# Gate columns of six feed-forward groups as seven quarter products instead of eight

## The chip, the cores and the metric

One core of one Trainium2 chip runs the whole layer as one program. The metric is device time in microseconds, the median of three runs.

## The reference, cut to what matters

One decoder layer on 512 tokens of width 1024 in float32: a modulated norm, two attention mixers that share an input projection, an output projection, and then a gated feed-forward part. The change touches the last part alone:

```
h = rms_norm(x, g_ffn_norm) * (1 + sc_f) + sh_f            # 512 x 1024
g_ff, u_ff = split(h @ w_gate_up, 2)                       # w_gate_up: 1024 x 5632
x = x + gt_f * ((silu(g_ff) * u_ff) @ w_down)              # 2816 hidden columns
```

`gt_f` is one of six vectors made from the condition `c`: `silu(c) @ w_mod + b_mod`, split in six.

## The kernel before, in words

Every float32 product is made of three matmuls in the `fp32r` type: each operand x is split into a high part (a cast, on ScalarE, ACT below) and a low part (x minus the high part, on VectorE, DVE below), and `mm3` (line 166) adds high times high, high times low and low times high in PSUM. `main3` (line 550) is `mm3` followed by `step()`, which lets the recording layer put in work of other engines.

**The order.** The program is written once, by Python generators ("tasks") and a small cost table (`Clocks`) that estimates when each engine comes to each instruction. `step()` puts in a piece of a task when the estimate says that its inputs are ready. What comes out is one fixed order for each engine; on the chip every engine runs its own order from front to back and waits on semaphores. So an instruction that waits holds up all that stands behind it on its engine, whether that needs the same thing or not.

**The feed-forward part.** The 2816 hidden columns are 11 groups of 256, `gi` = 0 to 10. A group has gate columns and up columns, each as two blocks of 128 features (f = 0, 1 gate, f = 2, 3 up) by 512 tokens, features on the partitions. The weights of a group come in four chunks of 256 rows (`gate_up_src`, line 1162; gate and up side by side): `wload` (line 176) loads a chunk into a tile `st` (three of them), ACT casts it to `wh`, DVE subtracts to `wl` (`split` inside `drive`, line 584; three `wh` and three `wl` tiles). A chunk is loaded as soon as the tile that it takes comes free, some two chunks ahead of TensorE. TensorE (PE) runs 24 matmuls of 512 tokens for each chunk: 4 blocks, 2 slices of 128 rows, 3 matmuls. Group 0 (`first_up`) is cut along the tokens, 256 at a time. Its weights were split early, into `O` tiles. Even groups collect in four PSUM banks `psacc`, odd ones in `pss`, two `pstr` and `pspv`.

**After a group** (`up_done`, line 1314) ACT takes silu of the gate blocks and DVE multiplies the up blocks in. `combine` (line 1268) then makes what the down projection needs, which was already done with seven products for eight (sums and differences of 256-token halves): four blocks for the first half of the products, kept in `g`, `K` or `O` tiles, and three for the second half, which are written to HBM as `second{gi}` by a DMA on the POOL queue and fetched later.

**The vector gt_f** is made beside groups 1 and 2 (`gtf_task`, line 1379; `mod_rows`, line 1009; `column_sums`, line 934), in two halves of 512 columns. Each half loads eight row blocks of `w_mod` in four DMAs into the same three `st` tiles that the weights use, and DVE adds them up in eight instructions (`cg<-st,cs,cg`). The sum is split into high and low parts, `gu` tiles, and two matmuls with a vector of ones add over the partitions (`pstr<-gu,oner`). These two matmuls have a fixed place in PE's order, between matmuls of the fourth chunk of group 1 (first half) and of the third chunk of group 2 (second half of the vector). If the `gu` tiles are late there, PE waits.

The functions that the change touches:

Of the kernel before, what the change touches and what calls it, by code (L numbers as in the profile page):

```python
# [115 lines left out]
def layer(ctx, tc, x, vecs, w_mod, w_in, gvecs, w_br_dsa, w_br_moba, w_out, w_gate_up, w_down, cosh, sinh, cosi, sini, out):  # L117
# [430 lines left out]
    emptied_next = [False]  # L548

# [34 lines left out]
    def drive(chunks, ws, ahead=2):  # L584
# [17 lines left out]
        def prep(c):  # L602

            early = c < len(chunks) and chunks[c][3]

            def load_next():
                if c + 1 < len(chunks) and chunks[c + 1][3]:
                    yield room("st"), lambda: block_room()
# [87 lines left out]
    sqj = cp.tile([P, HD], F32, name="sqj")  # L696
# [570 lines left out]

    def combine(gi, a0, a1):
# [10 lines left out]
        ve.tensor_tensor(out=s4, in0=a1[:, first], in1=a0[:, other], op=ALU.subtract)  # L1279
        if gi < 4:  # L1280
            yield a0, s13, room("g", 4)
            tiles = [t("g", [P, 2, 256], F32R) for _ in range(4)]
            ha, la, hb, lb = tiles
        else:
            tag = "K" if gi < 8 else "O"
            yield a0, s13, room(tag)
            tiles = [t(tag, [P, 4, 2, 256], F32R)]
# [8 lines left out]
        pair_tiles[gi] = tiles  # L1296
        pairs[gi] = {"A11": (ha[:, 0], la[:, 0]), "S2": (ha[:, 1], la[:, 1]), "S1": (hb[:, 0], lb[:, 0]),
                     "S3": (hb[:, 1], lb[:, 1])}
        ready.add(f"pair{gi}")
# [12 lines left out]
        ready.add(f"stored{gi}")  # L1312

    def up_done(gi):
        half = {}
# [49 lines left out]

    units = first_up()
    chunks.append((None, units[:4], ("h2_0", "h2_1"), None))
    chunks.append((None, units[4:], ("h2_2", "h2_3"), None))
    for gi in range(1, NF // 2):
        chunks += group([gate_up_src(gi, k2) for k2 in range(4)], 512, other_four if gi % 2 else four(),  # L1370
                        feat_mm(lambda k: (h2[k // 4][:, k % 4, :], h2[2 + k // 4][:, k % 4, :])), [0, 2, 1, 3],
                        up_done(gi))
# [51 lines left out]
    def earliest(*tags):  # L1424
        return lambda: min([min(free[tag]) for tag in tags if free[tag]], default=None)

# [15 lines left out]
    def split_first_half(loaded):  # L1442
# [3 lines left out]
        t2 = t(min((tag for tag in ("sc", "s") if free[tag]), key=lambda tag: min(free[tag])), [P, 512])  # L1446
# [40 lines left out]
    def second_task():  # L1487

        for q in range(NPAIR):
            yield (f"stored{NPAIR - 1}", "down",  # L1490
                   lambda: min([min(free[tag]) for tag in ("K", "O") if free[tag]], default=None))
            tag = min((tag for tag in ("K", "O") if free[tag]), key=lambda tag: min(free[tag]))
            x = t(tag, [P, 6, 256], F32R)
            pool_dma(x, second_acts[q])
            pairs[q] = {n: (x[:, a], x[:, 3 + a]) for a, n in enumerate(("A12", "A22", "S4"))}
# [162 lines left out]

    for second, load_of, split_of in ((False, load_first_half, split_first_half), (True, load_second_half, split_second_half)):
# [3 lines left out]
    with tc.manual_schedule(engines=engines):  # L1663
# [27 lines left out]
        spawn(gtf_task())  # L1691
        spawn(second_task(), slack=8.0, rank=0, on=(DVE,))
# [49 lines left out]
```

## Time and profile before

| | |
|---|---|
| median of 3 runs | 772.85 us (772.16 to 773.34) |
| the profiled execution | 771.89 us, of which the span from the first to the last instruction is 770.1 us |
| PE busy | 762.7 us, 99% of the span |
| weight loads (PEld) | 633.7 us, beside PE |
| DVE busy | 543.9 us, 71% |
| ACT busy | 394.4 us, 51% |
| granted TensorE clock | 1.00 throughout, the 2.4 GHz level |
| DMA | 126.59 MB, 164 GB/s over the span |

The profiled execution is one run with the hardware profiler; its span is the time between the first and the last instruction, and its own device time is 1.8 us more. A "busy" time adds up instructions that overlap only once. Matmuls are pipelined, so a single matmul's duration in a row is longer than the time that it adds; the time that one adds is read from the stretch of many in a row.

### The profile page before, as it was taken

What the parts mean: (1) busy time and instruction counts of PE and PEld (TensorE: products, weight loads), DVE (VectorE), ACT (ScalarE), POOL (GpSimd) and SP (SyncE); (2) the same over time, 40 slices, a digit from 0 to 9 for tenths busy, and PEclk for the clock granted to TensorE, in tenths of its full rate; (3) what the DMA queues carried; (4) which work ended last, traced back from release to release, by engine and by line L of the source; (5) the groups of instructions that cost most, each with busy time, mean ns of one, the idle gap of its engine ahead of it and who ended that gap; (6) DMA issues with size and microseconds to landing.
All of it is one profiled execution on the core that took longest, in us unless ns stands there. A gap on an engine that the chain in (4) does not pass through costs nothing.

```text
span 770.1 us, 10321 instructions
## 1 busy us (share of the span) xinstructions
PE 762.7 (99%) x3668; PEld 633.7 (82%) x3668; DVE 543.9 (71%) x1035; ACT 394.4 (51%) x835; POOL 48.3 (6%) x65
## 2 busy tenths in 40 slices
PE   8999999999999999999999999999999999999998
PEld 7787888888788887888888988888888888888886
DVE  6974889989799796337857277645444445897797
ACT  6763786779777756643435333333323323554341
POOL 2000012011111000000000000000000000012100
PEclk9999999999999999999999999999999999999999
DMA  9976352542035455433440257533444443479992
GB/s 319 333 227 228 84 170 78 165 134 58 29 83 193 149 163 194 151 109 123 139 149 1 83 185 251 178 124 101 132 150 124 150 150 138 160 256 381 331 319 83
DMA packets 84559, 126.59 MB, mean 164 GB/s; under 512 B 8976, under 2 KB 49240, under 8 KB 84508
## 3 DMA queue, kind: packets, MB, share of 16 engines
q1 hardware_dynamic: 80460, 105.75, 43.2%
q0 software_dynamic: 4048, 20.19, 7.5%
q8 instruction: 29, 0.48, 0.3%
q14 instruction: 22, 0.18, 0.1%
HBM read 112.28 MB, written 13.64 MB: 164 GB/s over the span
## 4 chain that ended last, share of the span: by engine, by line
PE 95%; SPq 2%; DVE 1%; DMA 1%; issue 0%; ACT 0%; ACTq 0%
PE psacc L110 62%; PE pstr L110 15%; PE pspv L110 9%; PE pss L110 9%; SPq L183 1%; DMA K<-in_w_mod_dram 1%; SPq L212 1%; DVE V L110 1%; DVE s L110 1%; SPq L221 0%; ACT gu L110 0%; ACT H L110 0%; SPq L205 0%; ACT acol L110 0%; ACT mcol L110 0%
## 5 line engine op out<-in xcount | busy, mean ns | idle before, releaser
L110 PE MATMUL psacc<-H,wh 128*128 128x512 f32 x576 | 182.8, 398 | 0.0
L110 DVE TENSOR_TENSOR wl<-st,wh 128x1024 fp32r<-128x1024 f32 (+1 forms) x110 | 128.5, 1168 | 61.1 <-ACT wh L110 60.9
L110 ACT CAST wh<-st 128x1024 fp32r<-128x1024 f32 (+1 forms) x110 | 110.4, 1005 | 76.3 <-PE psacc L110 32.6
L110 PE MATMUL psacc<-wh,H 128*128 128x512 f32 x384 | 126.5, 400 | 0.9 <-ACT H L110 0.9
L110 PEld LDWEIGHTS psacc<-H,wh 128*128 128x128 f32 x576 | 106.0, 188 | 22.3 <-issue 2.2
L110 PE MATMUL psacc<-H,wl 128*128 128x512 f32 x288 | 112.5, 390 | 0.0
L110 PEld LDWEIGHTS psacc<-wh,H 128*128 128x128 f32 x384 | 71.9, 188 | 16.8 <-ACT H L110 1.9
L110 PE MATMUL psacc<-wl,H 128*128 128x512 f32 x192 | 71.0, 390 | 0.0
L110 PEld LDWEIGHTS psacc<-H,wl 128*128 128x128 f32 x288 | 54.0, 188 | 11.7
L110 PE MATMUL pstr<-H,wh 128*128 128x512 f32 (+1 forms) x176 | 54.3, 390 | 0.0
L110 POOL TENSOR_TENSOR m<-m,mhalf 128x4 f32<-128x4 f32 (+1 forms) x24 | 28.6, 1193 | 390.5 <-DVE m L110 356.5
L110 PEld LDWEIGHTS psacc<-wl,H 128*128 128x128 f32 x192 | 36.1, 188 | 6.8
L110 PE MATMUL psacc<-O,wh 128*128 128x512 f32 x128 | 39.4, 389 | 0.0
L110 PEld LDWEIGHTS pstr<-H,wh 128*128 128x128 f32 (+1 forms) x176 | 32.3, 183 | 7.6
L110 ACT ACTIVATE s<-s,att 128x256 f32<-128x256 f32 (+3 forms) x64 | 34.2, 563 | 4.0 <-DVE att L110 3.7
L110 PE MATMUL pstr<-H,wl 128*128 128x512 f32 (+1 forms) x88 | 34.3, 390 | 0.0
L110 DVE TENSOR_TENSOR s<-psacc,s 128x512 f32<-128x512 f32 x12 | 8.2, 691 | 36.9 <-PE psacc L110 36.9
L110 PE MATMUL psacc<-H,O 128*128 128x256 f32 (+1 forms) x234 | 33.8, 303 | 0.0
L110 PEld LDWEIGHTS psacc<-H,O 128*128 128x128 f32 x234 | 31.0, 191 | 1.6
L110 PEld LDWEIGHTS psacc<-O,wh 128*128 128x128 f32 x128 | 24.0, 188 | 5.0
L110 ACT CAST H<-st 128x512 fp32r<-128x512 f32 (+1 forms) x21 | 16.1, 766 | 20.8 <-PE psacc L110 20.3
L110 ACT ACTIVATE s<-psacc 128x512 f32<-128x512 f32 x12 | 7.1, 596 | 37.2 <-PE psacc L110 37.2
(310 smaller groups left out, 1466.1 us busy)
## 6 DMA issues: line engine op xcount, KB each, us to landing
st<-in_w_gate_up_dram SPq DMA_DIRECT2D x88, 256.0 KB, 4.6
st<-in_w_in_dram SPq DMA_DIRECT2D x36, 512.0 KB, 3.6
K<-in_w_mod_dram SPq DMA_DIRECT2D x12, 1024.0 KB, 6.0
st<-in_w_down_dram SPq DMA_DIRECT2D x22, 512.0 KB, 4.8
second<-O POOLq DMA_DIRECT2D x11, 768.0 KB, 5.3
K<-in_w_mod_dram SPq DMA_DIRECT2D x16, 512.0 KB, 6.0
K<-second POOLq DMA_DIRECT2D x6, 768.0 KB, 9.3
st<-in_w_in_dram SPq DMA_DIRECT2D x16, 256.0 KB
```

Of the source, the lines that this page charges most:

```text
L110: inst = f(*args, **kw)
L183: last_dma[0] = nc.sync.dma_start(st[:, :, o:o + n], src.rearrange("(k p) n -> p k n", p=P))
L212: nc.sync.dma_start(strip[:, m], wmv[:, :, m * D + k * P:m * D + (k + 1) * P])
```

## The change

For groups 4 to 9 (`QUARTERS`) the gate columns are computed by a Strassen-like scheme with seven products. The 512 rows of a weight chunk are two halves, the 256 gate columns two halves, and the 512 tokens two halves of 256. Four blocks T1 to T4 of the tokens (sums and differences) are made once, in `token_task`, and kept in the four `K` tiles as high and low parts. For every chunk `split_quarters` makes from the gate weights the blocks A11, A12, A22 and the sums S1 to S4, as high and low parts in two `O` tiles. `quarter_chunks` runs the seven products, each 128 features by 256 tokens, two products in the halves of one PSUM bank, and `emptied` adds the banks to the four quarters of the gate result; silu then runs from SBUF. The up columns of such a group are plain products (`up_chunks`). A group's four chunks are now two of 512 gate rows and two of 512 up rows.

```diff
+    QUARTERS = range(4, 10)
+    def split_quarters(st):
+        v = st.rearrange("p k (f d) -> p k f d", f=2)
+        a11, a21, a12, a22 = v[:, 0:2, 0], v[:, 0:2, 1], v[:, 2:4, 0], v[:, 2:4, 1]
...
+        ve.tensor_tensor(out=p12[:, 0], in0=a21, in1=a22, op=ALU.add)
+        ve.tensor_tensor(out=p12[:, 1], in0=p12[:, 0], in1=a11, op=ALU.subtract)
+        ve.tensor_tensor(out=p34[:, 0], in0=a11, in1=a21, op=ALU.subtract)
+        ve.tensor_tensor(out=p34[:, 1], in0=a12, in1=p12[:, 1], op=ALU.subtract)
+        for x, sl in blocks[2:]:
+            se.copy(h[:, sl], x)
+        yield
+        for x, sl in blocks:
+            ve.tensor_tensor(out=l[:, sl], in0=x, in1=h[:, sl].bitcast(F32), op=ALU.subtract)
...
+    quarter_products = [("M1", "A11", "B11", 0, 0), ("M5", "S1", "T1", 0, 1), ("M2", "A12", "B21", 1, 0),
+                        ("M6", "S2", "T2", 1, 1), ("M7", "S3", "T3", 2, 0), ("M3", "S4", "B22", 3, 0),
+                        ("M4", "A22", "T4", 3, 1)]
...
+            for q, (n, x, b, at, p) in pieces:
+                ah, al = w[0][x][q]
+                last = a == 1 and q == qs[-1]
+                emptied_next[0] = last
+                main3(accs[at][:, 256 * p:256 * p + 256], ah, al, *token_block(b, a, q),
+                      a == 0 and q == 0 and not p, last, True)
```

The four `K` tiles and the `O` tiles are thereby taken, so the other users of them move. The four first-half blocks of groups 4 to 8 (`STAGED`) go to HBM as `first{gi}` and come back into `K` and `O` after group 9's gate columns. All blocks on their way to HBM, those of `second{gi}` for every group too, are now made in the weight tiles `wh` and `wl` (`staging`), and go out in two DMAs, one for the high and one for the low parts, where before they were made in an `O` tile and went out in one.

```diff
+    STAGED = range(4, 9)
+    def staging(n):
+        uid[0] += 1
+        return [wp.tile([P, n, 256], F32R, name=f"w{q}_{uid[0]}", tag="w" + q) for q in "hl"]
+    def first_task():
+        for q in STAGED:
+            yield f"staged{q}", "sums_done", earliest("K", "O")
+            tiles = [t(soonest("K", "O"), [P, 2, 4, 256], F32R)]
+            pool_dma(tiles[0], first_acts[q])
...
+        elif staged:
+            yield a0, s13
+            h, l = staging(4)
...
+        if staged:
+            first_acts[gi] = dp.tile([P, 2, 4, 256], F32R, name=f"first{gi}")
+            for n, q in enumerate((h, l)):
+                pool_dma(first_acts[gi][:, n], q, out_of=q)
...
-        yield s4, a1, room("O")
+        yield s4, a1
...
-        x = t("O", [P, 6, 256], F32R)
-        se.copy(x[:, 0:2], v1)
-        se.copy(x[:, 2], s4)
-        yield x
-        ve.tensor_tensor(out=x[:, 3:5], in0=v1, in1=x[:, 0:2].bitcast(F32), op=ALU.subtract)
-        ve.tensor_tensor(out=x[:, 5], in0=s4, in1=x[:, 2].bitcast(F32), op=ALU.subtract)
+        h, l = staging(3)
+        se.copy(h[:, 0:2], v1)
+        se.copy(h[:, 2], s4)
+        yield h
+        ve.tensor_tensor(out=l[:, 0:2], in0=v1, in1=h[:, 0:2].bitcast(F32), op=ALU.subtract)
+        ve.tensor_tensor(out=l[:, 2], in0=s4, in1=h[:, 2].bitcast(F32), op=ALU.subtract)
...
-        second_acts[gi] = dp.tile([P, 6, 256], F32R, name=f"second{gi}")
-        pool_dma(second_acts[gi], x, out_of=x)
-        done(x)
+        second_acts[gi] = dp.tile([P, 2, 3, 256], F32R, name=f"second{gi}")
+        for n, q in enumerate((h, l)):
+            pool_dma(second_acts[gi][:, n], q, out_of=q)
```

What this does to the order is read from the built program. The numbers behind a name tell tiles apart.

On DVE, around the end of group 0 and group 1, before: `wl_826` is the third chunk of group 1, `wl_834` its fourth, `wl_837` the first of group 2; `cg_816` is the first half of the vector; the two `O_832` rows write what becomes `second0`.

```order
L110 TENSOR_TENSOR wl_826_4450<-st_813_4337,wh_826_4449 128x1024
L110 TENSOR_TENSOR g_829_4460<-s_814_4394,g_828_4459 128x512
L110 TENSOR_TENSOR g_831_4462<-gu_824_4436,g_830_4461 128x512
L110 SCALAR_TENSOR_TENSOR cg_816_4418<-st_819_4423,cs_99,cg_816_4418 128x512
L110 TENSOR_TENSOR O_832_4470<-s_815_4409,O_832_4470 128x512
L110 TENSOR_TENSOR O_832_4470<-gu_825_4437,O_832_4470 128x256
L110 SCALAR_TENSOR_TENSOR cg_816_4418<-st_819_4423,cs_99,cg_816_4418 128x512
L110 TENSOR_TENSOR wl_834_4500<-st_827_4453,wh_834_4499 128x1024
L110 SCALAR_TENSOR_TENSOR cg_816_4418<-st_833_4476,cs_99,cg_816_4418 128x512 x2
L110 SCALAR_TENSOR_TENSOR cg_816_4418<-st_836_4512,cs_99,cg_816_4418 128x512
L110 TENSOR_TENSOR wl_837_4536<-st_835_4506,wh_837_4535 128x1024
```

The same place now: `wl_840` is the third chunk of group 1, `wl_845` its fourth, `wl_849` the first of group 2, `cg_826` the vector, and the two `wl_841` rows write what becomes the low part of `second0`.

```order
L111 TENSOR_TENSOR K_812_4273<-sc_822_4417,K_812_4273 128x512
L111 TENSOR_TENSOR g_837_4481<-s_824_4425,g_836_4480 128x512
L111 TENSOR_TENSOR g_839_4483<-gu_834_4467,g_838_4482 128x512
L111 TENSOR_SCALAR cg_826_4450<-st_828_4453,cs_99 128x512
L111 TENSOR_TENSOR wl_840_4487<-st_821_4356,wh_840_4486 128x1024
L111 TENSOR_TENSOR wl_841_4498<-s_825_4440,wh_841_4497 128x512
L111 TENSOR_TENSOR wl_841_4498<-gu_835_4468,wh_841_4497 128x256
L111 SCALAR_TENSOR_TENSOR cg_826_4450<-st_829_4455,cs_99,cg_826_4450 128x512 x2
L111 TENSOR_TENSOR wl_845_4546<-st_842_4506,wh_845_4545 128x1024
L111 SCALAR_TENSOR_TENSOR cg_826_4450<-st_843_4524,cs_99,cg_826_4450 128x512 x2
L111 SCALAR_TENSOR_TENSOR cg_826_4450<-st_844_4540,cs_99,cg_826_4450 128x512 x2
L111 TENSOR_TENSOR wl_849_4583<-st_846_4552,wh_849_4582 128x1024
```

Moved: instructions of `token_task` (17 ahead of the rows shown, in the time of group 0, and the `K_812` row) stand before the group's own, the weight tile `wl_845` takes the memory that `wl_841` had, so that its two instructions (cast and subtraction) wait for the DMAs that carry `wh_841` and `wl_841` out, and the first chunk of group 2 is loaded into the tile that `wl_845` empties (before, into one that a `cg` instruction had emptied).

On DVE, at the end of the vector's second half in group 2, before and then now; `wl_865` and `wl_875` are the fourth chunk of group 2, `cg_846` and `cg_856` the vector, `gu_868` and `gu_878` the low part that PE waits for, and the `O_863` and `wl_873` rows write what becomes `second1`.

```order
L110 TENSOR_TENSOR O_863_4658<-s_844_4587,O_863_4658 128x512
L110 TENSOR_TENSOR O_863_4658<-gu_855_4620,O_863_4658 128x256
L110 SCALAR_TENSOR_TENSOR cg_846_4593<-st_856_4628,cs_99,cg_846_4593 128x512 x2
L110 TENSOR_TENSOR wl_865_4688<-st_858_4638,wh_865_4687 128x1024
L110 SCALAR_TENSOR_TENSOR cg_846_4593<-st_864_4678,cs_99,cg_846_4593 128x512 x2
L110 TENSOR_TENSOR gu_868_4713<-cg_846_4593,gu_867_4712 128x512
```

```order
L111 TENSOR_TENSOR wl_873_4694<-s_854_4622,wh_873_4693 128x512
L111 TENSOR_TENSOR wl_873_4694<-gu_865_4655,wh_873_4693 128x256
L111 SCALAR_TENSOR_TENSOR cg_856_4628<-st_866_4663,cs_99,cg_856_4628 128x512 x2
L111 TENSOR_TENSOR wl_875_4725<-st_868_4673,wh_875_4724 128x1024
L111 SCALAR_TENSOR_TENSOR cg_856_4628<-st_874_4715,cs_99,cg_856_4628 128x512 x2
L111 TENSOR_TENSOR gu_878_4750<-cg_856_4628,gu_877_4749 128x512
```

The rows stand in the same order; what differs is that `wl_875` takes the memory of `wl_873` and so waits for the DMA that carries it to HBM, and `cg` and `gu` stand behind it. The two matmuls that read `gu` keep their place on PE: before and now they stand behind 18 matmuls of group 2's third chunk.

On PE, the start of group 4, before (`wh_891` is the first chunk, gate and up) and now (`O_904`, `O_905` are the high and low parts of the gate blocks, `K_812` is T1, `K_813` is T2).

```order
L110 MATMUL psacc_897_4937<-H_757_3943,wh_891_4881 128x512
L110 MATMUL psacc_897_4937<-H_759_3945,wh_891_4881 128x512
L110 MATMUL psacc_897_4937<-H_757_3943,wl_891_4882 128x512
L110 MATMUL psacc_899_4939<-H_757_3943,wh_891_4881 128x512
L110 MATMUL psacc_899_4939<-H_759_3945,wh_891_4881 128x512
```

```order
L111 MATMUL psacc_915_5012<-H_757_3943,O_904_4918 128x256
L111 MATMUL psacc_915_5012<-H_759_3945,O_904_4918 128x256
L111 MATMUL psacc_915_5012<-H_757_3943,O_905_4919 128x256
L111 MATMUL psacc_915_5012<-K_812_4273,O_904_4918 128x256 x2
L111 MATMUL psacc_915_5012<-K_812_4273,O_905_4919 128x256
L111 MATMUL psacc_916_5013<-H_757_3943,O_904_4918 128x256
```

A group's gate columns were 48 matmuls of 512 tokens and are 84 of 256.

## Rows read from the trace of the kernel before

**Rows 1.** The page: the span, busy us and share, GB/s moved in 40 slices.

```profile
span 770.1 us, 10321 instructions
PE 762.7 (99%) x3668; PEld 633.7 (82%) x3668; DVE 543.9 (71%) x1035; ACT 394.4 (51%) x835; POOL 48.3 (6%) x65
...
GB/s 319 333 227 228 84 170 78 165 134 58 29 83 193 149 163 194 151 109 123 139 149 1 83 185 251 178 124 101 132 150 124 150 150 138 160 256 381 331 319 83
```

**Rows 2.** The chain that ended last, in order of time: start, us, what.

```profile
423.80 19.07 PE psacc L110 x159
...
552.82 21.76 PE psacc L110 x96
```

**Rows 3.** Windows, group 6: busy us and count of PE, PEld, DVE, ACT, POOL.

```profile
552.00:573.80 21.80, 21.80 (x98) 18.06 (x97) 10.06 (x15) 7.20 (x11) 0.53 (x1) 1.00 0.43 133
```

**Rows 4.** Instruction groups by form on DVE from 419 to 760 us: busy, mean ns.

```profile
L110 DVE TENSOR_TENSOR wl<-st,wh 128x1024 fp32r<-128x1024 f32 x44 | 53.8, 1222 | 33.5 <-ACT wh L110 33.3
L110 DVE TENSOR_TENSOR O<-s,O 128x512 fp32r<-128x512 f32 x14 | 9.6, 686 | 0.5 <-ACT O L110 0.5
L110 DVE TENSOR_TENSOR gu<-s,s 128x256 f32<-128x256 f32 x22 | 9.3, 425 | 0.7
```

**Rows 5.** Timeline of DVE, 427 to 480 us: start, us, what, idle time before.

```profile
427.37 1.22 DVE L110 TENSOR_TENSOR wl<-st,wh 128x1024 fp32r<-128x1024 f32 x1 [0.26 <-ACT wh L110]
441.54 0.69 DVE L110 TENSOR_TENSOR s<-psacc,s 128x512 f32<-128x512 f32 x1 [12.94 <-PE psacc L110]
...
449.83 0.42 DVE L110 TENSOR_TENSOR O<-gu,O 128x256 fp32r<-128x256 f32 x1
...
450.97 1.22 DVE L110 TENSOR_TENSOR wl<-st,wh 128x1024 fp32r<-128x1024 f32 x1
...
458.90 1.22 DVE L110 TENSOR_TENSOR wl<-st,wh 128x1024 fp32r<-128x1024 f32 x1
...
465.58 0.49 DVE L110 TENSOR_SCALAR cg<-st,cs 128x512 f32<-128x512 f32 x1 [0.79 <-DMA st<-in_w_mod_dram]
...
473.10 0.42 DVE L110 TENSOR_TENSOR O<-gu,O 128x256 fp32r<-128x256 f32 x1
...
475.43 1.23 DVE L110 TENSOR_TENSOR wl<-st,wh 128x1024 fp32r<-128x1024 f32 x1 [0.46 <-ACT wh L110]
477.15 1.54 DVE L110 SCALAR_TENSOR_TENSOR cg<-st,cs,cg 128x512 f32<-128x512 f32 x2 [0.50 <-DMA st<-in_w_mod_dram]
479.43 0.69 DVE L110 TENSOR_TENSOR gu<-cg,gu 128x512 fp32r<-128x512 f32 x1 [0.74 <-ACT gu L110]
```

**Rows 6.** Timeline of ACT, cast of group 1's fourth chunk: start, us, what, idle before.

```profile
449.89 1.05 ACT L110 CAST wh<-st 128x1024 fp32r<-128x1024 f32 x1 [2.69 <-DMA st<-in_w_gate_up_dram]
```

**Rows 7.** Timeline of PE at the two places of the vector's matmuls.

```profile
463.13 0.63 PE L110 MATMUL pstr<-gu,oner 128*128 128x512 f32 x2
...
479.95 0.73 PE L110 MATMUL pstr<-gu,oner 128*128 128x512 f32 x2
```

**Rows 8.** Timeline of SP's DMA issues: start, us, what.

```profile
446.34 0.89 SPq L183 DMA_DIRECT2D st<-in_w_gate_up_dram  x2
...
450.94 0.90 SPq L183 DMA_DIRECT2D st<-in_w_gate_up_dram  x2
...
461.12 6.60 SPq L183 DMA_DIRECT2D st<-in_w_mod_dram  x3
```

**Rows 9.** Timeline of POOL's DMA issues: start, us, what, idle time before.

```profile
450.56 0.72 POOL L1257 DMA_DIRECT2D second<-O  x1 [28.97 <-DVE O L110]
```

**Rows 10.** DMA issues, 449 to 457 us: KB, median us to landing.

```profile
second<-O POOLq DMA_DIRECT2D x1, 768.0 KB, 5.3
```

**Rows 11.** DMA issues, 630 to 760 us: KB, median us to landing.

```profile
K<-second POOLq DMA_DIRECT2D x6, 768.0 KB, 9.3
...
sums<-sc POOLq DMA_DIRECT2D x6, 256.0 KB, 2.3
sums<-s POOLq DMA_DIRECT2D x5, 256.0 KB, 8.1
```

More of the change, by code (lines that the diff above doesn't have):

```diff
@@ L693, in rope @@
         done(u)
-    sqj = cp.tile([P, HD], F32, name="sqj")
+    m1 = cp.tile([P, 256], F32, name="m1")
+    sqj = m1[:, :HD]
     tabs = {}
@@ L1364, in first_up, with token_task, block, part @@
         return units
+    QUARTERS = range(4, 10)
+    token_sums = {}
+    def token_task():
+        yield ("h2_0", "h2_1", "h2_2", "h2_3", room("K", 4))
+        for n in range(1, 5):
+            token_sums[f"T{n}"] = t("K", [P, 2, 4, 256], F32R)
+        for a in range(2):
+            hb, lb = h2[a].bitcast(F32), h2[2 + a].bitcast(F32)
+            def block(q, r, c):
+                return q[:, 2 * r:2 * r + 2, 256 * c:256 * c + 256]
+            def part(n, x):
+                dst = token_sums[f"T{n}"][:, :, 2 * a:2 * a + 2]
+                se.copy(dst[:, 0], x)
+                yield dst
+                ve.tensor_tensor(out=dst[:, 1], in0=x, in1=dst[:, 0].bitcast(F32), op=ALU.subtract)
+            def difference(u, r, c, r2, c2):
+                v = t("sc", [P, 2, 256])
+                ve.tensor_tensor(out=u, in0=block(hb, r, c), in1=block(hb, r2, c2), op=ALU.subtract)
+                yield
+                ve.tensor_tensor(out=v, in0=block(lb, r, c), in1=block(lb, r2, c2), op=ALU.subtract)
+                yield
+                ve.tensor_tensor(out=u, in0=u, in1=v, op=ALU.add)
+                done(v)
+            yield room("sc", 2)
+            u = t("sc", [P, 2, 256])
+            yield from difference(u, 0, 1, 0, 0)
+            yield u
+            yield from part(1, u)
+            done(u)
+            yield room("sc", 2)
+            u = t("sc", [P, 2, 256])
+            yield from difference(u, 1, 1, 0, 1)
+            yield u
+            yield from part(3, u)
+            for n, op in ((2, ALU.add), (4, ALU.subtract)):
+                for q in (hb, lb):
+                    x = block(q, 0 if n == 2 else 1, 0)
+                    if n == 4 and q is hb:
+                        ve.tensor_tensor(out=u, in0=x, in1=u, op=ALU.subtract)
+                    else:
+                        ve.tensor_tensor(out=u, in0=u, in1=x, op=ALU.add)
+                    yield u
+                yield from part(n, u)
+            done(u)
+        ready.add("token_sums")
@@ new lines, in silus, with up_chunks, unit, load @@
+    def silus(half):
+        for f in range(2):
+            yield half[f]
+            se.activation(half[f], half[f], AF.Silu)
+    def up_chunks(gi, half):
+        accs = {}
+        fin = up_done(gi, half)
+        def unit(w, a, ks, fs):
+            if not accs:
+                for f, tag in enumerate(("s", "pv")):
+                    need_room("ps" + tag)
+                    accs[f] = ps(tag)
+            held_back[0] = 1.0 if a else 0.0
+            for k, f in [(k, f) for f in fs for k in ks] if a else [(k, f) for k in ks for f in fs]:
+                last = a == 1 and k == ks[-1]
+                emptied_next[0] = last
+                fs_ = slice(f * P, (f + 1) * P)
+                main3(accs[f], w[0][:, k, fs_], w[1][:, k, fs_], h2[a][:, k, :], h2[2 + a][:, k, :],
+                      a == 0 and k == 0, last)
+                emptied_next[0] = False
+                if last:
+                    fin(2 + f, accs[f])
+                    done(accs[f])
+                    step()
+        def load(c):
+            return lambda: wload([w_gate_up[c * 512:c * 512 + 512, DFF + gi * 256:DFF + gi * 256 + 256]], 4, 256)
+        return [(load(0), [lambda w, ks=ks: unit(w, 0, ks, (0, 1)) for ks in ((0, 1), (2, 3))], (), None),
+                (load(1), [lambda w, f=f: unit(w, 1, (0, 1, 2, 3), (f,)) for f in range(2)], (), None)]
@@ L1369, in layer @@
     for gi in range(1, NF // 2):
+        if gi in QUARTERS:
+            half = {}
+            chunks += quarter_chunks(gi, half) + up_chunks(gi, half)
+            continue
         chunks += group([gate_up_src(gi, k2) for k2 in range(4)], 512, other_four if gi % 2 else four(),
```

117 lines of the change are left out of this document (99 added, 18 removed).

## The prediction

> **What bounds the kernel now.** The page first: TensorE (PE) is busy for 762.7 of 770.1 us [rows 1]. Then the chain that ended last, in order of time. In the feed-forward part it is PE alone, and two of its rows give the prices: 96 matmuls of 512 tokens (one group) take 21.76 us, or 226.7 ns each; 159 matmuls of 256 tokens take 19.07 us, or 119.9 ns each [rows 2]. So a 256-token matmul costs 53% of a 512-token one, and narrowing loses 13 ns for each pair. The windows give the cover: in a steady group of 21.80 us DVE is busy for 10.06 and ACT for 7.20, PE all the time, at a granted clock of 1.00 [rows 3]. PE never waits here, so the change is worth the matmul time that it removes, less the time that PE is made to wait. The timelines of DVE, ACT, SP and POOL say who is close to being late.
>
> **The matmuls.** A gate half of a group was 48 x 226.7 ns = 10.88 us and becomes 84 x 119.9 ns = 10.07 us [rows 2]. Six groups save 6 x 0.81 = 4.85 us. That is 0.63% and the most that this change can give.
>
> **Work beside them.** In a changed group two splits of 1024 elements (2 x 1.22 us) leave DVE, and two quarter splits come in: four sums of 256 (0.425), three low parts of 512 (0.686) and one of 256, so 4.2 us each. The banks add one instruction of 512 and five of 256, 2.8 us [rows 4]. DVE goes from 10.06 to about 10.06 - 2.4 + 8.4 + 2.8 = 18.8 us of a group that now takes 20.95. ACT gains two casts of 512 and 256 elements a split and one copy, and stays under 11. Both remain hidden, DVE by only 2 us a group: without that cover each further us on DVE in a group is a us on PE, and the splits stand two chunks ahead, so it takes several such groups before PE feels it. I price this at nothing.
>
> The token sums T1 to T4 run once. Their first 17 DVE instructions, 17 x 0.686 = 11.7 us, fall into group 0, where DVE waited 12.94 us for PE [rows 4, 5]. Four of them wait for a cast on ACT (about 0.6 us each), so I let them end 1.2 us past the old wait. The rest lies in group 3 with five us and more in hand.
>
> **Where PE can be made to wait.** The blocks that go to HBM are now made in weight tiles, so a later weight split waits until its tile's DMA has landed. No such wait is in the trace of before: there the same bytes left from an `O` tile, and 768 KB took 5.3 us to land [rows 10]. Now 384 KB for the low part leaves alone, some two us behind the high part. The nearest rows are that 5.3 and 2.3 for 256 KB [rows 11]; both are bounds. A straight line through the two gives 3.05 us for 384 KB, their middle is 3.8. I choose 3.7, near the middle, because the loads around 450 us are as dense as they were beside the 5.3.
>
> Followed through, each step against the row of before:
> - The low part of `second0` was ready at 450.25 (449.83 + 0.42) and left at 450.56 [rows 5, 9]. With group 0's end 1.2 us late, less 0.75 that DVE then waited anyway, it leaves at 451.0 and lands at 454.7.
> - The split of group 1's fourth chunk began at 450.97 [rows 5]. It needs that tile: 454.8 to 456.0. PE needs it at 459 (its matmuls with the vector stand 4.1 us into the chunk, at 463.13 [rows 7]). No wait.
> - The load of group 2's first chunk was issued at 450.94 [rows 8]; it now takes the `st` tile that this split empties, so 456.1. From issue to the cast a like load took 449.89 - 446.34 = 3.55 us [rows 6, 8]. Cast 1.05 and split 1.22 more: 461.9, where before it ended at 460.12 [rows 5]. The low part of the vector's first half comes behind it, at 462.6, against 463.13. No wait, with half a us in hand.
> - The first load of the vector's second half, issued at 461.12 and first used at 465.58 [rows 5, 8], goes out at 462.0: 0.9 us late.
> - `second1`'s low part was ready at 473.52; now 474.4, left by 474.75, landed by 478.45. The split of group 2's fourth chunk began at 475.43 and has to wait for it: 478.55, so 3.1 us late.
> - Behind it on DVE stand the last two steps of the sum and `gu`. From that split to the end of `gu` it took 480.12 - 475.43 = 4.7 us, 0.5 of which was a wait that falls away: 482.7. PE's two matmuls on `gu` started at 479.95 and had nothing in hand [rows 5, 7]. PE waits about 2.5 us, and all that stands behind the two matmuls shifts with it.
>
> Each us of landing time counts about twice, once for `second0` and once for `second1`. At 2.3 us the wait is gone, at 5.3 it is 2.5 + 2 x 1.6 = 5.7.
>
> The Trainium skill weighs in on this term ("DMA: Bandwidth & Descriptors", the section on the anatomy of one DMA on the gpsimd path): it fits 2.0 us plus bytes over 436 GB/s, which makes 2.9 us for 384 KB, and 3.8 for 768 KB where the row shows 5.3. By it the wait would be 2.5 - 1.6 = 0.9 us and the gain 3.9; the row speaks for more, since the queue is not empty there.
>
> **The other places.** In groups 5 and 6 the second up chunk is split into a tile that has just sent out 512 KB. That store leaves some 5.4 us into the group: a multiply of 0.69, a split of 1.22, four steps of 0.425 and two low parts of 0.69 [rows 4], and half a us between them and to the issue. With 5.3 to land and 1.2 to split it is 12, and PE needs it at 10.07 + 24 x 0.2267 = 15.5. I price it at nothing; up to 8.8 us of landing it costs nothing. From group 9's gate columns on, five tiles of 1 MB come back on POOL's queue, and `second9` leaves behind them. The split of group 10's fourth chunk waits for that store. From the first fetch, at the end of group 9's gate columns, PE needs that split after 10.9 + 16.3 = 27 us, so the store by some 24. The 5.2 MB and 0.8 MB then ask for 250 GB/s. The core has moved up to 381 GB/s in a slice [rows 1], and group 10's own loads ask for about 0.5 MB in 5.44 us, 96 GB/s. I take nothing, and up to 5 us at the pace of the down projection, below.
>
> **The sum.** -4.85 + 2.5 = -2.35 us. The profiled execution was 771.89, which is 0.96 below the median of the runs, 772.85; so 769.5 for an execution like it and 770.5 for the median, 0.3% faster.
>
> **The rivals.**
> - **The stores land quickly**, in about 2.3 us as 256 KB did [rows 11]. Nothing waits, all 4.85 us arrive: 768.0. For it: no loads are as large as the one of 768 KB was. Against it: four loads of 512 KB share those ten us.
> - **The wait eats the gain**: a part store takes as long as a whole one did, 5.3 us. PE waits 5.7 us at the vector's second half, perhaps one at its first: net +0.9, 773.7, no change to be measured. For it: nothing in hand at 479.95 [rows 7]. Against it: half the bytes.
> - **Slower: the fetches of `first4` to `first8` stop group 10.** If POOL's queue moves less than 250 GB/s, `second9` lands late, the fourth chunk's split with it, and PE stands. In the down projection that queue has one fetch of 768 KB and one store of 256 KB for each 24 matmuls, 1.05 MB in 5.44 us or 193 GB/s; at that pace 6.0 MB take 31 us, 7 more than there are, and some 5 of them reach PE: 770.5 + 5 = 775.5. For it: 9.3 us for a fetch of 768 KB there, 8.1 for a store of 256 KB [rows 11]. Against it: that pace was all that was asked for, and SP's loads ran at the same time.
> - **DVE is the bound.** 18.8 of 20.95 us leaves 2 us for its waits on ACT; if it takes 22 us a group, six groups lose 6 us, of which the lead of two chunks takes most. Net near zero, 772.
>
> **How the numbers follow.** The forecast with its wait of 1 to 4 us: 769.0 to 772.0, chance 0.45, of which three quarters are faster. Quick landing, 0.20: faster. Eaten gain or DVE at its limit, 0.20: no change, some of it slower. Fetches in the way, 0.15: slower. A measurement of this kernel can tell 0.2%, 1.5 us, from no change. Faster by more: 0.33 + 0.19 = 0.52; within: 0.30; slower: 0.18. The range leaves out the ends of the first and the slower case: 767.8 to 774.8.
>
> **What would show it.** PE's gate stretches of groups 4 to 9 take 10.1 us each, 252 matmuls in three groups in 30.2: wrong, if a 256-token matmul with its operands in `K` and `O` costs more than 120 ns. In the waits, DVE's split of the fourth chunk of groups 1 and 2 waits for a DMA of `second`, and PE shows one gap of 1 to 4 us ahead of `pstr<-gu,oner` in group 2 and none, or a small one, in group 1. No gap in groups 5, 6 and 10. Wrong would be: gaps in several groups (DVE), a gap at group 10's fourth chunk (fetches), or a longer gap at the vector than 4 us (landing).

## The result and the profile after

The changed kernel takes 777.51 us (median of 7 runs, 775.50 to 778.87) against 773.34 us for the kernel before beside it (7 runs): 1.0055 times as long, 95% interval 1.0037 to 1.0072. It is slower, outside the range of 767.8 to 774.8, and on the other side from the forecast. The profiled execution took 778.61 us with a span of 776.8.

The page of the changed kernel, the span and the busy us and share of each engine:

```profile
span 776.8 us, 10981 instructions
PE 761.9 (98%) x3884; PEld 641.6 (83%) x3884; DVE 603.7 (78%) x1183; ACT 412.6 (53%) x885; POOL 62.2 (8%) x91
```

Against [rows 1], PE is busy for 0.8 us less, though six groups should have saved 4.85, and it is idle for 7.5 us more (14.9 for 7.4). So something eats the gain twice, by idle time and by matmuls that take longer.

The waits of PE from 415 us on (releaser, us in total, times, longest); in the kernel before there was none in this stretch:

```profile
PE pstr L111 <- DVE s L111: 3.2, 1, 3.2
PE pstr L111 <- ACT gu L111: 2.0, 1, 2.0
PE psacc L111 <- DVE g L111: 1.2, 1, 1.2
PE pstr L111 <- DVE gu L111: 0.2, 1, 0.2
```

The timeline of PE at these places (start, us, what, idle before):

```profile
463.15 0.39 PE L111 MATMUL pstr<-H,wl 128*128 128x512 f32 x1
466.73 0.73 PE L111 MATMUL pstr<-gu,oner 128*128 128x512 f32 x2 [3.19 <-DVE s L111]
...
468.06 1.05 PE L111 MATMUL pspv<-H,wh 128*128 128x512 f32 x2
468.91 0.63 PE L111 MATMUL pspv<-H,wl 128*128 128x512 f32 x1
469.34 1.05 PE L111 MATMUL psacc<-H,wh 128*128 128x512 f32 x2
...
472.32 0.62 PE L111 MATMUL psacc<-H,wh 128*128 128x512 f32 x2
...
487.42 0.49 PE L111 MATMUL pstr<-gu,oner 128*128 128x512 f32 x1 [2.02 <-ACT gu L111]
```

PE stops at both halves of the vector, not at one [rows 7]. Behind the stop, a step of two matmuls and one takes 1.28 us (468.06 to 469.34) where it takes 0.68 otherwise: 427 ns for each matmul of 512 tokens against 227. It does so for some 3.5 us behind each stop, which costs 1.6 and 1.5 us more. The granted clock is 0.50 there, the 1.2 GHz level (windows, as in [rows 3]; the clock is the third number from the end):

```profile
468.00:471.00 3.00, 3.00 (x8) 2.31 (x7) 2.03 (x5) 1.05 (x1) 0.00 (x0) 0.50 0.76 251
488.60:491.10 2.50, 2.50 (x7) 1.97 (x6) 2.50 (x4) 0.00 (x0) 0.00 (x0) 0.50 0.64 195
```

Why PE stops is in the timeline of DVE (at 447 us and on, to be laid beside [rows 5]) ...

```profile
447.74 1.22 DVE L111 TENSOR_TENSOR wl<-st,wh 128x1024 fp32r<-128x1024 f32 x1
...
450.48 1.53 DVE L111 SCALAR_TENSOR_TENSOR cg<-st,cs,cg 128x512 f32<-128x512 f32 x2
458.35 1.22 DVE L111 TENSOR_TENSOR wl<-st,wh 128x1024 fp32r<-128x1024 f32 x1 [6.34 <-DMA second<-wl]
459.49 3.10 DVE L111 SCALAR_TENSOR_TENSOR cg<-st,cs,cg 128x512 f32<-128x512 f32 x4
464.25 1.23 DVE L111 TENSOR_TENSOR wl<-st,wh 128x1024 fp32r<-128x1024 f32 x1 [1.65 <-ACT wh L111]
465.39 0.68 DVE L111 TENSOR_TENSOR gu<-cg,gu 128x512 fp32r<-128x512 f32 x1
465.99 0.68 DVE L111 TENSOR_TENSOR s<-pstr,s 128x512 f32<-128x512 f32 x1
```

... of ACT, and of SP (its issues, [rows 8] before):

```profile
456.57 1.05 ACT L111 CAST wh<-st 128x1024 fp32r<-128x1024 f32 x1 [7.25 <-DMA second<-wh]
...
482.96 1.05 ACT L111 CAST wh<-st 128x1024 fp32r<-128x1024 f32 x1 [6.28 <-DMA second<-wh]
```

```profile
442.65 3.99 SPq L1017 DMA_DIRECT2D sc<-in_vecs_dram  x2
448.99 0.89 SPq L184 DMA_DIRECT2D st<-in_w_gate_up_dram  x2
449.97 2.43 SPq L184 DMA_DIRECT2D st<-in_w_mod_dram  x2
```

The split of group 1's fourth chunk begins at 458.35, not at 450.97, and what stands behind it (the vector's steps, the split of the next chunk, `gu`) is late with it. The DMA issues of 449.5 to 451.2 us (KB, us to landing) show the store it waited for:

```profile
second<-wh POOLq DMA_DIRECT2D x1, 384.0 KB, 6.9
second<-wl POOLq DMA_DIRECT2D x1, 384.0 KB, 7.4
```

Half of the bytes took longer than the whole had [rows 10]. The SP rows give a reason that the prediction did not look for: the loads of the weights and of `w_mod` go at 448.99 and 449.97 instead of 446.34 and 447.47, into the store. Two things stand ahead of them. The vector's bias is loaded into the `sc` tiles, which the token sums now hold, and SP is not past those two loads until 446.64. Then the load of the fourth chunk waits 2.3 us more (waits of SP, 446.5 to 449.2 us):

```profile
SPq L184 <- DVE wl L111: 2.3, 1, 2.3
```

It takes the tile that the split of the third chunk empties (447.74 to 448.96, first row of DVE above), and that split now stands behind rows of the token sums and of group 0. Before, it took a tile that a step of the vector's sum emptied at 446.32 (DVE and SP, before):

```profile
445.57 0.75 DVE L110 SCALAR_TENSOR_TENSOR cg<-st,cs,cg 128x512 f32<-128x512 f32 x1
447.47 0.37 SPq L183 DMA_DIRECT2D st<-in_w_mod_dram  x1
```

The list of what moved, in the section on the change, does not have this load.

Last, the windows of group 4's 84 gate matmuls and of a steady group (us, busy us and count of PE, PEld, DVE, ACT, POOL, clock, DMA share, GB/s; [rows 3] before):

```profile
518.68:528.76 10.08, 10.08 (x86) 10.07 (x85) 9.41 (x18) 5.73 (x11) 1.07 (x2) 1.00 0.56 176
552.00:572.95 20.95, 20.95 (x133) 19.06 (x132) 17.32 (x36) 9.70 (x19) 2.12 (x4) 1.00 0.58 190
```

The gate half takes 10.08 us, and DVE is busy for 17.3 of 20.95 without PE waiting.

**A ruler for all runs.** The first product of the feed-forward part (`psacc<-H,O`) begins between 418.1 and 420.5 us, and two profiles of the kernel before differ by 1.5 us there (418.74 and 420.22), so this is not the change. In the six profiles that begin it after 420.0 us the granted clock was 0.50 from 17.3 to 20.0 us of the span, in the other ten 1.00. The table takes two differences of starts on PE's timeline: from that product to the first matmul of the down projection (`pstr<-wh,g`), and from there to the end of the last matmul.

| profile | up part, us | down part, us |
|---|---|---|
| before | 242.71 | 104.95 |
| before, again | 243.14 | 105.09 |
| changed | 247.34 | 106.77 |
| changed, again | 244.56 | 104.95 |
| O tile | 239.27 | 107.16 |
| staging alone | 245.23 | 104.95 |
| late slot | 245.04 | 106.87 |
| O tile, two halves | 239.31 | 105.96 |
| sums in g | 242.24 | 107.47 |
| O tile, fetch late | 238.21 | 107.90 |
| all three | 237.92 | 104.95 |
| all three, again | 238.08 | 104.95 |
| three groups | 241.46 | 107.78 |
| paced fetches | 237.91 | 108.60 |
| O tile, half fetches | 238.19 | 104.95 |
| all three, half fetches | 237.91 | 105.02 |

### The profile page after: what moved, and what is told of

Its sections match the earlier page's. It is cut to its first block, busy times and chain, and to the rows that moved or that the text cites. A ratio compares the mean times of both kernels' runs of the same rounds, so it can differ in the third digit from the quotient of the medians.

```text
span 776.8 us, 10981 instructions
## 1 busy us (share of the span) xinstructions
PE 761.9 (98%) x3884; PEld 641.6 (83%) x3884; DVE 603.7 (78%) x1183; ACT 412.6 (53%) x885; POOL 62.2 (8%) x91
## 4 chain that ended last, share of the span: by engine, by line
PE 60%; issue 17%; DVE 10%; DMA 7%; SPq 2%; ACT 2%; POOL 2%; POOLq 0%; DVEq 0%; ACTq 0%
PE psacc L111 43%; PE pstr L111 8%; PE pspv L111 5%; PE pss L111 5%; DMA st<-in_w_down_dram 3%; DVE wl L111 2%; DMA second<-wl 2%; DVE H L111 2%; DVE s L111 2%; DVE sc L111 1%; SPq L184 1%; POOL second L1260 1%; DMA K<-in_w_mod_dram 1%; DVE pT L111 1%; DMA second<-wh 1%
## 5 line engine op out<-in xcount | busy, mean ns | idle before, releaser
L111 PE MATMUL psacc<-H,wh 128*128 128x512 f32 x384 | 125.6, 409 | 0.0
L111 PEld LDWEIGHTS psacc<-H,wh 128*128 128x128 f32 x384 | 71.3, 192 | 15.4 <-issue 2.1
L111 PE MATMUL psacc<-H,wl 128*128 128x512 f32 x192 | 75.8, 395 | 0.0
L111 PE MATMUL psacc<-H,O 128*128 128x256 f32 (+1 forms) x459 | 71.2, 295 | 1.2 <-DVE g L111 1.2
L111 PEld LDWEIGHTS psacc<-H,O 128*128 128x128 f32 x459 | 62.8, 191 | 4.0 <-DVE g L111 1.6
L111 PE MATMUL psacc<-K,O 128*128 128x256 f32 x288 | 43.4, 283 | 0.0
L111 PE MATMUL pspv<-H,wh 128*128 128x512 f32 x128 | 39.9, 393 | 0.0
L111 PE MATMUL pss<-H,wh 128*128 128x512 f32 x128 | 39.5, 390 | 0.0
L111 PEld LDWEIGHTS psacc<-K,O 128*128 128x128 f32 x288 | 38.4, 192 | 0.0
L111 PEld LDWEIGHTS pspv<-H,wh 128*128 128x128 f32 x128 | 24.2, 189 | 5.1
```

What stands on the lines that cost most here:

```text
L111: inst = f(*args, **kw)
```

## The experiments

Medians are compared with the kernel before on the same chip: 772.99 to 773.10 us, 771.48 to 776.42 over all rounds.

### One thing undone, one thing alone

The second-half blocks of groups 0 to 2 in an `O` tile:

```diff
-        yield s4, a1
+        yield (s4, a1) + ((room("O"),) if gi < 3 else ())
...
-        h, l = staging(3)
+        if gi < 3:
+            x = t("O", [P, 2, 3, 256], F32R)
+            h, l = x[:, 0], x[:, 1]
+        else:
+            h, l = staging(3)
...
+        if gi < 3:
+            pool_dma(second_acts[gi], x, out_of=x)
```

> The changed kernel, with one thing undone: the second-half blocks of groups 0 to 2 are made in an O tile again and leave in one DMA; the order on every engine is the same as in the changed kernel. Theory of the tiles (the weight split waits for the store of second0 and second1, PE stops at the vector's two matmuls, and after each stop runs at half clock for a while): no stop at either place, the six gate stretches give their 4.85 us, so 768 us, 1.1 to 1.3% below the changed kernel and 0.6% below the kernel before. Rival, the token sums: they hold the sc tiles that the bias of the vector is loaded into, and so hold up SP's loads (448.99 for 446.34); if that stops PE, one stop of 1 to 3 us stays at the first half of the vector, and the time is 770 to 773.

770.64 us, 0.9964 times before (0.9951 to 0.9977): faster than both kernels, but 2.6 us over the 768 of the theory. Both long stops are gone (0.4 us stays at the first), and the up part is 8.1 us shorter than in the changed kernel. All waits of PE from 415 us on:

```profile
PE psacc L111 <- DVE g L111: 1.2, 1, 1.2
PE psacc L111 <- DVE wl L111: 0.6, 1, 0.6
PE pstr L111 <- DVE s L111: 0.3, 1, 0.3
```

So without the blocks in the weight tiles there is no long stop. The rest of the 4.85 is missing at two places that this edit does not touch: 0.7 us at group 10 and 2.2 in the down part.

The staging alone, put into the kernel before:

> The kernel before, with only the staging of the change: the second-half blocks of all groups are made in weight tiles and leave in two DMAs; no quarter products, no token sums. Theory of the tiles: both stops appear, 3.4 and 2.6 us, each with some 1.7 us at half clock behind it, so 782 us, 1.1 to 1.3% slower than before. Rival (it is the token sums, which hold up SP's loads until they meet the store, that made the store land after 7.4 us): here the loads go at their old times, half of the bytes land within the 5.3 us of the whole, and PE stops for 5 us at most, clock and all: 774 to 778.

775.29 us, 1.0034 (1.0018 to 1.0050), 2.2 us slower: not the 782 of the theory, but in the rival's range. The DMA issues and the waits of PE in this kernel:

```profile
second<-wh POOLq DMA_DIRECT2D x1, 384.0 KB, 4.0
second<-wl POOLq DMA_DIRECT2D x1, 384.0 KB, 4.3
```

```profile
PE pstr L110 <- DVE s L110: 1.1, 1, 1.1
PE pstr L110 <- ACT gu L110: 0.5, 1, 0.5
```

With SP's loads at their old times the store lands after 4.0 and 4.3 us, PE stops for 1.3 and 1.2 us more than before, the clock stays, and the up part is 2.52 us longer. In total that is the wait that the prediction priced at 2.5, from a landing of 3.7, but half of it falls on the vector's first half, where the prediction had none. So both theories hold a part: without the tiles no long stop, without the token sums two small ones.

The two matmuls of each half of the vector later on PE, nothing else edited:

```diff
-        yield parts + (room("pstr"), bias, lambda: ck.ready[parts[1].tensor.name][0] + 1.0)
+        yield parts + (room("pstr"), bias, lambda: ck.ready[parts[1].tensor.name][0] + (9.0 if bias_tag else 1.0))
```

> The changed kernel, with the two matmuls of each half of the vector put later in PE's order (by 33 matmuls, 7.5 us, for the first half, and 120, 27 us, for the second); the tiles and their waits stay. Theory: DVE and ACT still wait some 6 us for the stores of second0 and second1, but nothing that PE needs at once stands behind them, so PE has no stop: 768 to 769.5. Rival (the late splits themselves reach PE): a stop moves to the fourth chunk of group 1 or the first of group 2, 770 to 775.

774.89 us, 1.0025 (1.0011 to 1.0038). ACT still waits 6.0 and 5.5 us for the stores, and PE has no wait at all up to 505 us, as the theory says. But the vector now lets go of the `sc` tiles later, the token sums end later, and PE waits for them at group 4 (waits, 505 to 527 us):

```profile
PE psacc L111 <- ACT K L111: 2.7, 1, 2.7
PE psacc L111 <- DVE K L111: 1.2, 1, 1.2
```

The stop has moved. Behind it the clock fell once more: 23 matmuls of 256 tokens take 5.3 us from 520.88 on, 230 ns each for 120.

```profile
521.00:525.00 4.00, 4.00 (x19) 3.84 (x19) 3.90 (x8) 2.37 (x5) 0.95 (x2) 0.50 0.33 116
```

The up part is 7.1 us over the shortest (245.04 for 237.92), 4.3 of them the stop and 2.8 the slow matmuls. The time lies in the rival's range, but the stop came at a place that neither theory named.

### Why the store lands late

The run with the `O` tile, its store cut into two DMAs:

```diff
-            pool_dma(second_acts[gi], x, out_of=x)
+            for n in range(2):
+                pool_dma(second_acts[gi][:, n], x[:, n], out_of=x)
```

> As the run with the O tile, but the store of second0 to second2 leaves in two DMAs of 384 KB (high, low; rows of 3 KB for 6 KB). Nothing waits for it, so the time should be that of the run with the O tile, 768. What is asked is the landing. Theory that the form makes the store slow (half the row for each packet, so a smaller share of the DMA engines beside the loads): 6 to 7.5 us for each half, where the one DMA of 768 KB takes 5 to 5.5 beside the same loads. Rival (the loads that come later now meet the store): the one DMA of 768 KB in the run with the O tile is slower too, 7 us or more, and the halves here no slower than that.

769.99 us, the time of the other to the resolution. The halves of `second0` land after 3.5 and 5.3 us (the first leaves 2.5 us ahead of the second); the whole took 5.3 before, and in the run with the `O` tile:

```profile
second<-O POOLq DMA_DIRECT2D x1, 768.0 KB, 6.8
```

The form theory falls: rows of 3 KB were no slower here, and the whole store suffers too when SP's loads come later.

The token sums in `g` tiles, so that the bias loads go early (the second half of the sums also waits until the vector is done):

```diff
-                v = t("sc", [P, 2, 256])
+                v = t("g", [P, 2, 256])
...
-            yield room("sc", 2)
-            u = t("sc", [P, 2, 256])
+            yield room("g", 2)
+            u = t("g", [P, 2, 256])
...
-            yield room("sc", 2)
-            u = t("sc", [P, 2, 256])
+            yield (room("g", 2),) + (("gtf",) if a else ())
+            u = t("g", [P, 2, 256])
```

> The changed kernel, with one thing moved: the token sums use g tiles as scratch and leave the two sc tiles to the bias of the vector; the vector's matmuls keep their places on PE, the blocks stay in the weight tiles. Theory now (two causes multiply: the wait for the store, and the token sums that hold SP's queue until its loads meet the store): second0's stores land in 4 to 5 us for 6.9 and 7.4, the two stops are 0.5 to 1.5 us each as in the run with the staging alone, the clock does not fall, and the time is 772.85 - 4.85 + 2.5 + 1.8 (the down projection) = 772.3, that is 771.5 to 773.5. Rival (the tiles alone, whatever SP does): stops as in the changed kernel, 777.

775.10 us, 1.0021 (1.0003 to 1.0040), 770.8 to 778.5: between the two theories, a miss for both. SP's load goes at 448.55, which is 28.2 us behind group 0's start (27.6 before, 30.0 in the changed kernel). The landing of the stores and the waits of PE at the vector:

```profile
second<-wh POOLq DMA_DIRECT2D x1, 384.0 KB, 4.8
second<-wl POOLq DMA_DIRECT2D x1, 384.0 KB, 5.8
```

```profile
PE pstr L111 <- ACT gu L111: 1.7, 1, 1.7
PE pstr L111 <- DVE s L111: 1.6, 1, 1.6
```

From start to start of the matmuls the stops are 1.7 and 2.4 us, with the matmuls behind them at 227 ns. The low part leaves 31.8 or 31.9 us behind group 0's start in all of these kernels; it lands after 4.3 us with the load at 27.6 (the staging alone), 5.8 at 28.2 and 7.4 at 30.0. With the `O` tile, where nothing waits for it, the whole `second0` lands after 6.2 to 6.8 us in the three profiles with the sums in `sc` and after 5.1 to 5.8 in the five with the sums in `g`. So the landing goes with the place of the loads. The high part has a share in it too: in the run with two halves it left 1.2 us earlier, with the loads at 30.0, and the low part landed after 5.3.

Over the 237.92 us of an up part without stops, the changed kernel loses 9.4 and 6.6 us in its two profiles, this one 4.3 in its one, the staging alone 2.5 over before. So by these profiles the `sc` tiles cost 2.3 to 5.1 us, the waits by themselves 2.5, and some 1.8 are left that the token sums add in another way; which, is not shown.

### The down projection

In the changed kernel's first profile PE waits once more at some 730 us (list of waits above, `DVE g`), and the down part is 1.8 us longer. In the run with the `O` tile DVE shows this, 6 us ahead of the down projection (657.85):

```profile
651.45 1.23 DVE L111 TENSOR_TENSOR wl<-st,wh 128x1024 fp32r<-128x1024 f32 x1 [9.06 <-DMA second<-wl]
```

That is the split of group 10's fourth chunk, behind `second9`'s store, which is behind the five fetches. In the 48 us behind it DVE is idle for 0.4 us in all, so it never catches up: the load of `w_down` that SP issued 26.6 us into the down projection before (688.04 - 661.45), into a tile that DVE frees, now goes at 28.6 (686.46 - 657.85).

The fetches behind that store, in the run with the `O` tile:

```diff
-            yield f"staged{q}", "sums_done", earliest("K", "O")
+            yield f"staged{q}", f"stored{QUARTERS[-1]}", "sums_done", earliest("K", "O")
```

> The run with the O tile, with one thing moved: the five fetches of first4 to first8 go onto POOL's queue behind the stores of second9, not before them. Theory: the 9.06 us that DVE waited for second9 ahead of group 10's fourth chunk fall under 3 us, PE's stop there (0.8 us) goes, DVE begins the weights of the down projection some 2.5 us earlier, and the wait of 1.8 us that PE had 70 us later goes too: 770.6 - 2.5 = 768.1, range 767.5 to 769. Rival (the wait in the down projection comes from something else there, such as loads of w_down that land late beside the fetches of the second half): it stays, and the time is 769.5 to 770.5.

769.54 us, 0.9953 (0.9937 to 0.9968). The store lands after 4.8 us, DVE's wait ahead of the split falls to 5.2 (under 3 was expected), and the stop at group 10 is gone. But now the loads of the first blocks of `w_down` come late beside the fetches, DVE waits for two of them (0.75 and 0.68 us), the load still goes at 28.1 us, and PE waits for 2.9 us. The lateness came another way than I had expected.

All three edits:

> All three together: O tile for the second-half blocks of groups 0 to 2, token sums in g tiles, fetches of first4 to first8 behind second9. Theory: nothing left that PE waits for; the 4.85 us of the matmuls arrive whole: 767.5 to 768.3 for the median, 0.6 to 0.7% under the kernel before. Rival (part of the gain is lost in something not seen yet): 769 or more.

768.79 us, 0.9947 (0.9929 to 0.9964): the lowest median of the kernels that do the whole computation, though half a us over what was expected. In both of its profiles PE has no wait of note, and the parts sum to 4.79 us less than before, the 4.85 of the matmuls.

Quarters for groups 7 to 9 alone:

> As the run with all three together, but the quarter products for groups 7 to 9 alone, groups 4 to 6 as plain products. Theory: only the matmul time changes, three groups times 0.81 us: 2.4 us more than with six groups. Rival (a group of quarters costs DVE or ACT time that reaches PE): the difference is under 1.5 us.

771.51 us, 2.7 more than with six groups, where 2.4 were expected. Its profile has waits of 0.8 us at group 7 and 2.8 in the down part, so it doesn't price a group any closer than the ruler does.

The fetches spread over the down projection; the fetches of `second` now stand behind the last of them:

```diff
-            yield f"staged{q}", f"stored{QUARTERS[-1]}", "sums_done", earliest("K", "O")
+            yield (f"staged{q}", f"stored{QUARTERS[-1]}", "sums_done", earliest("K", "O")) + ((f"half{q - 4}",) if q > 4 else ())
...
-            yield f"stored{NPAIR - 1}", "down", earliest("K", "O")
+            yield f"stored{NPAIR - 1}", f"pair{STAGED[-1]}", "down", earliest("K", "O")
...
+            if not second:
+                ready.add(f"half{c}")
```

> As the run with all three together, but first5 to first8 are fetched one by one, each when the down projection is four pairs ahead of its use, instead of all five in a row at group 10. Only POOL's queue changes. Theory (the five fetches in a row make the first loads of the down projection late, DVE begins 1.0 to 1.6 us late against PE, SP's loads of w_down go 1.5 us later than in the kernel before, and PE waits 1 to 3 us some 60 us into the down projection): DVE's splits and SP's loads stand as in the kernel before (26.6, 31.9, 36.2, 40.5 us behind the start of the down projection), no PE wait there, 767.5 to 768.3. Rival (the wait there comes and goes with the execution, whatever the fetches do): the median stays at 768.8 and the spread at 3 us.

772.21 us, 0.9991 (0.9976 to 1.0005): worse than both theories had it. The up part is as short as any (237.91), the down part the longest (108.60). The early loads stand where they stood before, but DVE waits 1.8 and 3.3 us for two loads of `w_down`, the load at 26.6 us now goes at 28.6 and a later one at 37.2 for 31.9. Put into the down projection, the fetches do more harm.

Three kernels a second time:

> The kernel before, unchanged, for a second profile. Theory that the wait in the down projection belongs to the fetches: none here, the down projection takes 104.95 us from its first matmul to its last, as in the first profile, while the attention part may differ by 1 us. Rival (it comes and goes with the execution): a wait of 1 to 3 us here too.

> The changed kernel, unchanged, for a second profile. Theory: again two stops at the vector's matmuls, together with their slow clock 7 to 10 us, and a wait of 1 to 3 us in the down projection. Rival (the size of the stops is chance): stops of 1 to 2 us without the slow clock.

> The run with all three together, unchanged, for a second profile. Theory: no stop at the vector; in the down projection, where its DVE is 1 us late, between no wait and 2.9 us. If it is 104.95 us again, a lateness of 1 us is covered.

The kernel before (773.94) has no wait in its down projection; that it took 2 us more than its first profile is 1.5 ahead of the feed-forward part and 0.4 at the vector. The changed kernel (775.39) stops again at both places, 3.2 and 1.8 us more than the kernel before, the first again with the lower clock behind it and the second not; but it has no wait in the down projection. All three together (768.99): 104.95 us again. So the stops belong to the change, what they cost varies by some 3 us, and the wait in the down projection comes and goes in the changed kernel.

Half of each fetch, in the run with the `O` tile and in the one with all three. The low parts of `first4` to `first8` stay out, so these two kernels do not compute the layer:

```diff
-            pool_dma(tiles[0], first_acts[q])
-            (ha, hb), (la, lb) = ((tiles[0][:, n, 0:2], tiles[0][:, n, 2:4]) for n in range(2))
+            pool_dma(tiles[0][:, 0], first_acts[q][:, 0])
+            (ha, hb), (la, lb) = ((tiles[0][:, 0, 0:2], tiles[0][:, 0, 2:4]) for n in range(2))
```

> The run with the O tile, with half of each fetch left out: of first4 to first8 only the high parts (512 KB each, 2.5 MB in all) come back and stand in for the low parts too; same order, same tiles. Theory (the fetches hold up the store of second9 and the first loads of the down projection): DVE's wait for second9 falls from 9.1 us to 6 or less, PE's stop of 0.8 us at group 10 goes, SP's loads of w_down in the second half go at 26.6 to 27.3 us behind the start of the down projection for 28.1, and the wait of 1.8 us there is gone or under 0.5: 768 to 769 for the median, for 770.6. Rival (the fetches have no part in it): DVE's wait and the loads as in the run with the O tile, 770 to 771.

> The run with all three together, with half of each fetch left out in the same way (the high parts of first4 to first8 stand in for their low parts). Theory: the loads of w_down stand 0.8 us or less behind those of the kernel before, no wait in the down projection, 767.5 to 768.5, and the spread is that of the part before the first gate product alone (2.4 us). Rival: as with all three together, 768.8.

768.01 us (767.80 to 769.23), 0.9935 (0.9920 to 0.9949), and 768.21 us (767.23 to 771.22, a wider spread than expected). In both the load goes at 26.5 us, the down part takes 104.95 and 105.02 us, and in the first DVE's wait at group 10 is down to 4.2 us, as much as with the staging alone (its timeline):

```profile
647.97 1.23 DVE L111 TENSOR_TENSOR wl<-st,wh 128x1024 fp32r<-128x1024 f32 x1 [4.22 <-ACT wh L111]
```

So the fetches of `first4` to `first8` make DVE and the load late. Whether PE then waits goes with the place of that load, over all sixteen profiles: in the eight where it goes at 28.0 us or earlier the down part is at most 0.14 us over its shortest, in the eight where it goes at 28.1 or later 1.0 to 3.7 us. The changed kernel has 28.2 in its first profile and 28.0 in its second. Why so little tips it is not shown. With the wait at the vector and half of the fetches' weight off, no loss is left that these profiles show.

## Why the prediction was wrong, step by step

- **The matmuls, -4.85 us: right.** 10.08 us for a gate half, and 4.79 us for the up part with everything else out of the way (237.92 for 242.71).
- **DVE beside them, 18.8 of 20.95 us, priced at nothing: right.** 17.3 in the window shown, and no wait of PE in groups 5 to 9.
- **The token sums, 1.2 us on DVE and nothing more: here the prediction failed first.** As far as it went that came out: the low part of `second0` left at 450.87, 451.0 was forecast. But the sums were followed on DVE and ACT alone. They also take the two `sc` tiles and move the third chunk's split on DVE, and the loads on SP's queue move by 2.4 us against group 0 (30.0 for 27.6). That queue was not walked.
- **The landing, 3.7 us: the term that was mis-sized.** It was near for the queue as it stood (4.0 and 4.3 with the staging alone; that the up part then lost the 2.5 us of the sum is in part luck, since half of it came at the other place), and wrong for the one that the change makes: 6.9 and 7.4, then 5.9 and 6.1. I took 5.3, the landing of twice the bytes, for an upper end. It is none: in the same trace [rows 11] has 8.1 us for a store of 256 KB, and `second9` took longer than 5.3 (DMA issues, 640 to 648 us, before):

```profile
second<-O POOLq DMA_DIRECT2D x1, 768.0 KB, 6.8
```

  With a landing of 7.4 my own rows give a stop at the first half of 3.2 us; 3.4 were measured.
- **What a stop costs.** It was counted as its length. Behind the two stops PE ran at the lower clock, which cost 3.1 us together in the first profile (1.6 in the second, behind one stop) and stood in no term of the sum.
- **The fetches, priced at nothing, "up to 5 us".** The rival had the queue right and the place wrong: `second9` landed late, DVE waited 7.8 us for it, and PE felt it 70 us later, 1.8 us in this profile and none in the second.

The sum by the ruler: -4.79 + 9.42 + 1.82 = 6.45 us, and 0.24 that this execution began its feed-forward part later: 6.7, the difference of the spans (776.8 - 770.1). That is the profiled execution; by the medians the change costs 4.2 us where 2.35 were to be gained.

The Trainium skill ("DMA: Bandwidth & Descriptors", the section on the anatomy of one DMA on the gpsimd path) would by its fit, as an estimate, have 2.9 us for 384 KB. Where one load alone is issued beside the two stores, the trace agrees; the DMA issues of 523.9 to 526 us in the changed kernel:

```profile
second<-wh POOLq DMA_DIRECT2D x1, 384.0 KB, 2.6
second<-wl POOLq DMA_DIRECT2D x1, 384.0 KB, 3.0
```

At 450 us a store of the same size took 7.4. For one among loads the measurement decides.

## What to carry to other kernels

Before giving a buffer to a transfer, ask who takes that buffer next and what stands behind that on its engine: here a split that had time enough was followed by two matmuls that had none. A borrowed scratch tile counts on every queue that waits for it, the load queue above all. And price a store by the traffic in the microseconds in which it is under way, after the change has moved that traffic, with an upper end well above its landing today.

## What was not expected of the hardware

- A store of 384 KB landed after 2.6 us in one place and 7.4 in another of the same execution; one of 768 KB at the same place in the program after 5.3 or 6.8, by the loads beside it.
- The granted clock fell to 0.50, the 1.2 GHz level, for some 3.5 us behind stops of PE of 3.4, 3.2 and 2.2 us, and for almost 6 us behind two stops in a row of 2.9 and 1.4 us (the late slot); behind stops of 1.1 to 1.9 us (the down projection, the staging alone, the sums in `g`) it stayed at 1.00 and the matmuls went on at 227 ns.
